# Experts: the first 64 tokens of an expert as two parts of 32, the second in a conditional block

## The chip, the cores and the metric

One core of a Trainium2 chip runs the whole program. The metric is the device time of one execution in microseconds (us); of the kernel before there are three timed executions, and one more was profiled.

## The reference, cut to what matters

The program is two transformer blocks in float32 over 512 tokens of width 1024. The change lies in the last part, the mixture of experts, which with the closing norm takes the last 1,400 of the 2,390 us:

```python
logits = xt @ router_w + router_b             # 512 tokens, 32 experts
top_val, top_idx = lax.top_k(logits, 4)       # each token goes to 4 experts
gate = softmax(top_val)
for e in range(32):                           # x: the tokens that chose e
    gu = x @ w_gu[e] + b_gu[e]                # 1024 -> 2 x 1024, the way up
    g, up = min(gu[:, :1024], 7), clip(gu[:, 1024:], -7, 7)
    act = (up + 1) * (g * sigmoid(1.702 * g))
    y = act @ w_down[e] + b_down[e]           # 1024 -> 1024, the way down
    out[tokens of e] += gate * y
```

The number of tokens of an expert depends on the data. The reference's router, worked out on its inputs, gives for experts 0 to 31: 41, 14, 111, 66, 75, 197, 45, 40, 14, 80, 57, 61, 46, 61, 26, 50, 62, 135, 185, 22, 73, 58, 101, 74, 62, 102, 1, 26, 39, 41, 12, 71. Seven have 32 or fewer, thirteen have 33 to 64, six have 65 to 96, three have 97 to 128 and three have more.

## The kernel before, in words

**Weights.** Each expert has twelve slabs of 1 MB: eight of `w_gu` (one for each 128 rows) and four of `w_down`. `load` issues them on SP into a ring of 21 slots in the order gu(0), gu(1), dn(0), gu(2), dn(1), and so on, two in flight (`FLIGHT`). A load waits until the last reader of its slot is done. Counting 21 back, the load of dn(e,1), the second slab of expert e's way down, goes to the slot of gu(e,0): it waits until TensorE has left the conditional block of expert e's way up. By then dn(e,0) and everything ahead of it may have been loaded. The load of gu(e+2,5) likewise waits for the end of the way down of expert e-1.

**Products.** Tokens are the stationary operand, weights the moving one. In form `n=2` (`up`, `down`) 64 tokens are loaded as 64 columns, and the two halves of the output columns go to two halves of the array and of PSUM's partitions. In form `n=4` 32 tokens are loaded, and four quarters of the output columns go to the four quarters of the array. Every float32 product is two records in the trace, so that a way up is 64 records of 512 columns in either form, and a way down 32 records of 512 columns (`n=2`) or 64 of 256 (`n=4`). A bias product opens each sum. `swiglu` follows on VectorE and ScalarE.

**Parts and blocks.** Tokens 0 to 63 of each expert go unconditionally in form `n=2`. Tokens 64 to 95 and 96 to 127 go in form `n=4`, inside `tc.If(r > 64)` and, nested in it, `tc.If(r > 96)`; later 64s (`chunk`) in form `n=2` inside further nested blocks. `r` is the expert's count in a register of each engine. For more than 128 tokens the activations of later chunks go to DRAM (`spill`) on the way up and are fetched back (`late<-spill`, line 1744) on the way down. `hinted` sets a branch hint for TensorE ahead of each block.

**Order.** For each e: `tile_up(e)` (line 1687), then the transposes of the next expert's tokens, then `tile_down(e-1)` (line 1739), then the transposes of expert e's activations. Inside a stretch without branches a scheduler sets the order; it put two or three of the four slabs of the way down of e-1 ahead of the block of the way up of e (line 1710). The block of the way down is at line 1742, its inner ones at 1748 and 1732.

**GpSimd.** Its queue holds, in program order, the gathers of tokens (`xg`, `x`, `late`), the spills and their way back, and the scatters `acc<-y` (line 1620) that add a part's result to the output. Each scatter waits for the landing of the one before.

Of the kernel before, what the change touches and what calls it, by code (L numbers as in the profile page):

```python
# [68 lines left out]
def uid(g, s):  # L69
    g.n += 1  # L70
    return f"{s}_{g.n}"
# [1245 lines left out]
NCH = T // CH  # L1317
QUARTERS = 2
RING = 5, 16
# [7 lines left out]
class Moe:  # L1327
# [143 lines left out]
    def table(self, n, half):  # L1471

        g = self.g
        nc, V = g.nc, g.nc.vector
        w, m = P // n, 4 if n == 2 else QUARTERS
        d = self.rp.tile([3 * NE, 4, 2, CH], F32, tag="dup", bufs=2, name=uid(g, "dup")).rearrange("p c h s -> p (c h s)")[:, :m * P].rearrange("p (c h s) -> p c h s", h=n, s=w)
        first = 0 if n == 2 else CH
        src = self.ptab[half][:3 * NE, first:first + m * w].rearrange("p (c s) -> p c s", s=w)
        (nc.scalar.copy if n == 2 else V.tensor_copy)(d, src.unsqueeze(2).to_broadcast([3 * NE, m, n, w]))
        pr = tr_tile(g, uid(g, "ptab"))  # L1480
        for c in range(m):
            nc.tensor.transpose(pr[:, c * 96:(c + 1) * 96], d[:, c].rearrange("p h s -> p (h s)"), g.ident[:96, :96])
        pv = pr[:, :m * 96].rearrange("p (c j e) -> p c j e", j=3, e=NE)
        cs = slice(half * 4, half * 4 + m)
        e = self.rp.tile([P, 4, NE], F32, tag="emp", bufs=2, name=uid(g, "emp"))[:, :m]
# [21 lines left out]
    def buffers(self, ctx):  # L1507
# [6 lines left out]
        tile = lambda name: self.pool.tile([P, 512], F32, name=name)  # L1514
        self.x1, self.act1 = tile("x1"), [tile(f"act1{j}") for j in range(2)]
        self.late, self.T = [[tile(f"{x}{j}") for j in range(2)] for x in ("late", "turned")]
        for x in (self.x1, *self.act1, *self.late):
            self.g.nc.gpsimd.memset(x, 0.0)
# [76 lines left out]

    def down(self, n, e, c, aT, mid=None):

# [6 lines left out]
        if n == 2:  # L1604
            nc.tensor.matmul(py, self.sel[e], self.bias[:, 2, :], start=True, stop=False)
        else:
            aT = aT[:, c * nb:(c + 1) * nb]
            for odd in range(2):
                nc.tensor.matmul(py, self.quarters(e, odd), self.bias[:, 2, odd * N:(odd + 1) * N], start=not odd, stop=False)
        for k in range(KD):  # L1610
# [78 lines left out]
    def tile_up(self, e, xT):  # L1689
# [3 lines left out]
        g, tc, r, x = self.g, self.g.tc, self.r[e], self.late  # L1693
        act0, act1 = self.pool.tile([P, 512], F32, tag="act0", bufs=1, name=uid(g, "act")), self.act1[e % 2]
        more = self.hinted(e, CH, "up")
        self.up(2, e, xT, act0, mid=lambda: self.transposed(self.x1, self.turned(1)))

# [11 lines left out]

        with tc.If(r > CH, label=more):  # L1710
            with tc.If(r > 2 * CH):
                self.fetch(x[0], e, 2)
            more = self.hinted(e, CH + CH // 2, "up")
            self.up(4, e, self.turned(1), act1[:, 0:256], 0)
            with tc.If(r > CH + CH // 2, label=more):
                more = self.hinted(e, 2 * CH, "up")
                self.up(4, e, self.turned(1), act1[:, 256:512], 1, mid=lambda: self.transposed(x[0], self.turned(2)))
                chunk(2, more)
        return act0, act1

    def tile_down(self, e, aT, act1, more):
        g, tc, r, a = self.g, self.g.tc, self.r[e], self.late
        self.down(2, e, 0, aT, mid=lambda: self.transposed(act1, self.turned(1), 0.5))

# [16 lines left out]

        with tc.If(r > CH, label=more):  # L1742
            with tc.If(r > 2 * CH):
                g.nc.gpsimd.dma_start(a[0], self.spill[e % 2, 0])
                back(3)
            more = self.hinted(e, CH + CH // 2, "down")
            self.down(4, e, 0, self.turned(1))
            with tc.If(r > CH + CH // 2, label=more):
                more = self.hinted(e, 2 * CH, "down")
                self.down(4, e, 1, self.turned(1), mid=lambda: self.transposed(a[0], self.turned(2), 0.5))  # L1750
                chunk(2, more)

# [44 lines left out]
    def run(self):  # L1797
# [11 lines left out]
        for e in range(NE + 1):  # L1809
# [4 lines left out]
            if e:  # L1814
                more = self.hinted(e - 1, CH, "down")
            if e + 1 < NE:
# [5 lines left out]
            if prev is not None:  # L1822
                self.tile_down(e - 1, aT, prev[1], more)
                blk = block()
                self.load(KD // 2)
# [119 lines left out]
```

## Time and profile before

| | us |
|---|---|
| three timed executions, median (lowest to highest) | 2384.4 (2382.29 to 2391.74) |
| profiled execution, its own time | 2391.75 |
| its span, first to last instruction | 2389.9 |
| TensorE busy in the span | 2083.4 (87%) |
| VectorE, ScalarE, GpSimd busy | 860.2, 476.2, 329.0 |
| bytes moved, mean rate | 584.26 MB, 244 GB/s |

The expert stage runs from about 980 us to the last product at 2356 us; the closing norm follows. TensorE is the busiest engine, but in most of the stage the queues that load weights are busy nine tenths too, so a share says little here: what matters is which of the two waits for the other at each expert.

### The profile page before, as it was taken

The numbers are of one execution on the slowest core, as the hardware profiler recorded it, in microseconds if no ns is written. First come the engines' busy times: TensorE is split into PE (matmuls) and PEld (weight loads), VectorE is DVE, ScalarE is ACT, GpSimd is POOL, SyncE is SP. The second block draws the span as 40 slices with busy tenths as digits, with TensorE's granted clock in tenths as the row PEclk, the third lists the DMA queues.
The fourth block names the chain that finished last, engine by engine and source line by source line (L and its number), as shares of the span: only waits on it lengthen the run. The fifth ranks groups of instructions, "written<-read, shape, count | busy, mean of one in ns | idle before, by whom it ended". The sixth has DMA issues, their size and how long they took to land. (4 is left out here: it accounts for less than half of the span.)

```text
span 2389.9 us, 31193 instructions
## 1 busy us (share of the span) xinstructions
PE 2083.4 (87%) x11589; PEld 1140.7 (48%) x11589; DVE 860.2 (36%) x1891; ACT 476.2 (20%) x839; POOL 329.0 (14%) x329
## 2 busy tenths in 40 slices
PE   6999888999989999798998888776887989888873
PEld 6756765688878978433333333222233333333221
DVE  6466668755566556411120111111121122121112
ACT  3345332234433134001001000000000000100001
POOL 2000224400022211101101101001001110101002
PEclk9999989999999999799999999999998999999997
DMA  6442476752336617879749899999966698989995
GB/s 190 121 162 69 154 191 198 222 173 98 97 117 219 208 50 254 348 292 325 278 152 332 291 338 335 323 354 335 340 236 243 235 331 326 332 312 340 346 333 180
DMA packets 213971, 584.26 MB, mean 244 GB/s; under 512 B 32287, under 2 KB 107438, under 8 KB 179822
## 3 DMA queue, kind: packets, MB, share of 16 engines
q1 hardware_dynamic: 182688, 523.74, 61.9%
q0 software_dynamic: 16784, 46.94, 7.2%
q10 hardware_dynamic: 14142, 9.10, 1.3%
q8 instruction: 190, 3.11, 0.5%
q14 instruction: 167, 1.37, 0.2%
HBM read 537.88 MB, written 41.84 MB: 243 GB/s over the span
## 5 line engine op out<-in xcount | busy, mean ns | idle before, releaser
L1587 PE MATMUL pg<-wgu,xT 128*64 128x512 f32 x1024 | 316.9, 648 | 57.2 <-issue 32.1
L1587 PE MATMUL pu<-wgu,xT 128*64 128x512 f32 x1024 | 299.0, 620 | 0.0
L1614 PE MATMUL py<-wdn,aT 128*64 128x512 f32 x1024 | 239.7, 605 | 21.4 <-DMA wdn<-in_exp_w_down 17.7
L1547 DVE TENSOR_TENSOR turned<-ptx,cols 128x512 f32<-128x512 f32 x42 | 29.0, 692 | 498.5 <-PE ptx L1539 497.2
L1561 ACT ACTIVATE th<-gm 128x512 f32<-128x512 f32 (+1 forms) x54 | 30.2, 559 | 843.6 <-DVE gm L1560 843.6
L89 DVE TENSOR_TENSOR wlo<-wst,whi 128x1024 fp32r<-128x1024 f32 (+1 forms) x109 | 136.6, 1253 | 124.7 <-ACT whi L88 115.7
L88 ACT CAST whi<-wst 128x1024 fp32r<-128x1024 f32 (+2 forms) x121 | 123.9, 1027 | 257.0 <-DMA wst<-in_w_ff_in 69.6
L1587 PEld LDWEIGHTS pg<-wgu,xT 128*64 128x64 f32 x1024 | 74.8, 145 | 191.7 <-issue 142.1
L1587 PEld LDWEIGHTS pu<-wgu,xT 128*64 128x64 f32 x1024 | 84.8, 144 | 159.7 <-issue 159.7
L1614 PEld LDWEIGHTS py<-wdn,aT 128*64 128x64 f32 x1024 | 70.0, 138 | 164.7 <-issue 130.1
L1620 POOL DMA_INDIRECT acc<-y,idx x54 | 85.7, 1586 | 327.3 <-ACTq L1742 137.8
L1591 PE MATMUL pgu<-wgu,turned 128*32 128x512 f32 x1152 | 129.2, 597 | 0.0
L98 PE MATMUL pf<-hTh,whi 128*128 128x512 f32 (+1 forms) x288 | 112.1, 393 | 8.0 <-ACT whi L88 5.0
L100 PE MATMUL pf<-hTh,wlo 128*128 128x512 f32 (+1 forms) x288 | 110.3, 385 | 6.6 <-DVE wlo L89 6.6
L1531 POOL DMA_INDIRECT xg<-hn,idx x32 | 32.9, 1028 | 600.7 <-PE ptx L1539 551.5
L1539 PE MATMUL ptx<-ident,act 128*128 128x128 f32 x256 | 44.4, 301 | 80.9 <-PEq L1742 52.8
L99 PE MATMUL pf<-hTl,whi 128*128 128x512 f32 (+1 forms) x288 | 110.4, 384 | 0.0
L1654 DVE CAST sel<-pick 128x128 fp32r<-128x128 f32 x32 | 7.6, 236 | 272.1 <-PEq L1732 133.2
L1614 PE MATMUL py<-wdn,turned 128*32 128x256 f32 (+1 forms) x1280 | 99.9, 414 | 0.0
L99 PE MATMUL plt<-wlo,ahi 128*128 128x512 f32 x256 | 99.7, 389 | 0.0
L98 PE MATMUL plt<-whi,ahi 128*128 128x512 f32 x256 | 99.6, 389 | 0.0
L100 PE MATMUL plt<-whi,alo 128*128 128x512 f32 x256 | 99.2, 389 | 0.0
(541 smaller groups left out, 3428.2 us busy)
## 6 DMA issues: line engine op xcount, KB each, us to landing
wgu<-in_exp_w_gu SPq DMA_DIRECT2D x256, 1024.0 KB
wdn<-in_exp_w_down SPq DMA_DIRECT2D x128, 1024.0 KB
wst<-in_w_in SPq DMA_DIRECT2D x36, 512.0 KB
wst<-in_w_ff_in SPq DMA_DIRECT2D x32, 512.0 KB
wst<-in_w_ff_out SPq DMA_DIRECT2D x32, 512.0 KB
ada_w<-in_ada_w SPq DMA_DIRECT2D x24, 512.0 KB
a<-in_ada_w SPq DMA_DIRECT2D x24, 512.0 KB
wst<-in_w_out SPq DMA_DIRECT2D x16, 512.0 KB
```

Of the source, the lines that this page charges most:

```text
L88: g.nc.scalar.copy(hi, st)
L89: eng.tensor_tensor(out=lo, in0=st, in1=hi.bitcast(F32), op=ALU.subtract)
L98: g.nc.tensor.matmul(out, ah, bh, start=start, stop=False)
L99: g.nc.tensor.matmul(out, ah, bl, start=False, stop=False)
L100: g.nc.tensor.matmul(out, al, bh, start=False, stop=stop)
L1531: self.g.nc.gpsimd.indirect_dma_start(out=x, out_offset=None, in_=self.hn, in_offset=bass.IndirectOffsetOnAxis(ap=self.idx[2][:, c, e:e + ...
L1539: d = g.nc.tensor.transpose(pt[:, b * P:(b + 1) * P], x[:, b * P:(b + 1) * P], g.ident)
L1561: nc.scalar.activation(th, gm, AF.Tanh, scale=0.851)
L1587: nc.tensor.matmul(ps[h * w:(h + 1) * w, :], lhs, W[k][:, o + h * N:o + (h + 1) * N], start=False, stop=(k == KD - 1))
L1591: nc.tensor.matmul(both[h * w:(h + 1) * w], lhs, wk[:, h], start=False, stop=(k == KD - 1))
L1614: nc.tensor.matmul(py[h * w:(h + 1) * w, :], lhs, W[k // 2][:, o:o + N], start=False, stop=(k == KD - 1))
L1620: nc.gpsimd.indirect_dma_start(out=acc, out_offset=bass.IndirectOffsetOnAxis(ap=self.idx[n][:, c, e:e + 1], axis=0), in_=y, in_offset=None ...
```

## The change

`QUARTERS` becomes 4, so that tables of row numbers and gates in form `n=4` cover tokens 0 to 127. Tokens 0 to 31 go unconditionally in form `n=4`; tokens 32 to 63 go in form `n=4` inside a new block `tc.If(r > 32)`, in which the block for more than 64 is now nested. The transposes of tokens 64 to 127 move into the new block. `act0` becomes one fixed tile that is cleared once. The first product of a way down gets an ordering edge behind the block of the way up. The diff without the tables:

```diff
-        act0, act1 = self.pool.tile([P, 512], F32, tag="act0", bufs=1, name=uid(g, "act")), self.act1[e % 2]
-        more = self.hinted(e, CH, "up")
-        self.up(2, e, xT, act0, mid=lambda: self.transposed(self.x1, self.turned(1)))
+        act0, act1 = self.act0, self.act1[e % 2]
+        more = self.hinted(e, CH // 2, "up")
+        self.up(4, e, xT, act0[:, 0:256], 0)
...
-        with tc.If(r > CH, label=more):
-            with tc.If(r > 2 * CH):
-                self.fetch(x[0], e, 2)
-            more = self.hinted(e, CH + CH // 2, "up")
-            self.up(4, e, self.turned(1), act1[:, 0:256], 0)
...
+        with tc.If(r > CH // 2, label=more):
+            more = self.hinted(e, CH, "up")
+            self.up(4, e, xT, act0[:, 256:512], 1, mid=lambda: self.transposed(self.x1, self.turned(1)))
+            with tc.If(r > CH, label=more):
+                with tc.If(r > 2 * CH):
+                    self.fetch(x[0], e, 2)
+                more = self.hinted(e, CH + CH // 2, "up")
+                self.up(4, e, self.turned(1), act1[:, 0:256], 0)
...
-        self.down(2, e, 0, aT, mid=lambda: self.transposed(act1, self.turned(1), 0.5))
+        self.down(4, e, 0, aT, after=after)
...
-        with tc.If(r > CH, label=more):
-            with tc.If(r > 2 * CH):
-                g.nc.gpsimd.dma_start(a[0], self.spill[e % 2, 0])
-                back(3)
...
+        with tc.If(r > CH // 2, label=more):
+            more = self.hinted(e, CH, "down")
+            self.down(4, e, 1, aT, mid=lambda: self.transposed(act1, self.turned(1), 0.5))
+            with tc.If(r > CH, label=more):
+                with tc.If(r > 2 * CH):
+                    g.nc.gpsimd.dma_start(a[0], self.spill[e % 2, 0])
+                    back(3)
...
-                more = self.hinted(e - 1, CH, "down")
+                more = self.hinted(e - 1, CH // 2, "down")
-                self.tile_down(e - 1, aT, prev[1], more)
+                self.tile_down(e - 1, aT, prev[1], more, blk)
```

In the changed kernel line 1712 opens the new block of the way up and 1715 the one for more than 64; 1747 and 1750 are the same two of the way down.

What the change moves, first on TensorE at the end of a way up. This is expert 2 before, from its last two slabs (`wgu`) to its block at 1710; `wdn` is the way down of expert 1:

```order
L1587 MATMUL pg_10000<-wgu_9133,xT_9660 64x512 x2
L1587 MATMUL pu_10001<-wgu_9133,xT_9660 64x512 x2
L1587 MATMUL pg_10000<-wgu_9135,xT_9660 64x512 x2
L1587 MATMUL pu_10001<-wgu_9135,xT_9660 64x512 x2
L1679 COMPARE_AND_BRANCH
L1679 UNCONDITIONAL_BRANCH x2
L1614 MATMUL py_10548<-wdn_9137,aT_9986 64x512 x4
L1614 MATMUL py_10548<-wdn_9641,aT_9986 64x512 x4
L1710 COMPARE_AND_BRANCH
```

Two slabs of the way down stand ahead of the block. The same place on TensorE in the changed kernel:

```order
L1590 MATMUL pgu_10150<-wgu_9181,xT_9752 32x512 x4
L1590 MATMUL pgu_10150<-wgu_9183,xT_9752 32x512 x4
L1712 COMPARE_AND_BRANCH
L1688 REGISTER_ALU
L1949 BRANCH_PREFETCH_HINT
L1580 MATMUL pgu_10196<-bias,sel_8530 128x512 x2
L1590 MATMUL pgu_10196<-wgu_8587,xT_9752 32x512 x4
L1590 MATMUL pgu_10196<-wgu_9171,xT_9752 32x512 x4
L1590 MATMUL pgu_10196<-wgu_9173,xT_9752 32x512 x4
```

No slab of a way down is left ahead of the block, and the second part with its own hint stands in it.

Next the way down of expert 1 on TensorE, behind that block. Before, from the hint for the block at 1742 to that block:

```order
L1941 BRANCH_PREFETCH_HINT
L1539 MATMUL ptx_10496<-ident,xg_9668 128x128 x4
L1539 MATMUL ptx_10560<-ident,act_8534 128x128 x4
L1614 MATMUL py_10548<-wdn_9643,aT_9986 64x512 x4
L1614 MATMUL py_10548<-wdn_9645,aT_9986 64x512 x4
L1742 COMPARE_AND_BRANCH
```

Eight products (sixteen records) and eight transposes part the hint and its branch. In the changed kernel, up to the second hint:

```order
L1949 BRANCH_PREFETCH_HINT
L1538 MATMUL ptx_10691<-ident,xg_9760 128x128 x4
L1608 MATMUL py_10743<-bias,sel_8531 128x256 x2
L1616 MATMUL py_10743<-wdn_9185,aT_10137 32x256 x8
L1616 MATMUL py_10743<-wdn_9733,aT_10137 32x256 x8
L1616 MATMUL py_10743<-wdn_9735,aT_10137 32x256 x8
L1616 MATMUL py_10743<-wdn_9737,aT_10137 32x256 x8
L1747 COMPARE_AND_BRANCH
L1688 REGISTER_ALU
L1949 BRANCH_PREFETCH_HINT
```

All four slabs (32 products, 64 records of half the width) now stand between the hint and the branch, and the transposes of `act` have gone into the block.

Last the queue of GpSimd at the way down of expert 0, from the gather for expert 2 to the fetch that brings spilled activations back (`late<-spill`). Before:

```order
L1531 DMA xg_9668<-hn,idx_7703 128x512
L1620 DMA acc<-y_9696,idx_7703 1152x512
L1742 COMPARE_AND_BRANCH
L1743 COMPARE_AND_BRANCH
L1728 COMPARE_AND_BRANCH
L1729 DMA late_8536<-spill 128x512
L1728 UNCONDITIONAL_BRANCH
L1728 ISA
L1728 UNCONDITIONAL_BRANCH
L1744 DMA late_8535<-spill 128x512
```

One scatter stands ahead of the fetches. In the changed kernel:

```order
L1530 DMA xg_9760<-hn,idx_7703 128x512
L1622 DMA acc<-y_9799,idx_7704 2304x256
L1747 COMPARE_AND_BRANCH
L1622 DMA acc<-y_9847,idx_7704 2304x256
L1750 COMPARE_AND_BRANCH
L1751 COMPARE_AND_BRANCH
L1733 COMPARE_AND_BRANCH
L1734 DMA late_8539<-spill 128x512
L1733 UNCONDITIONAL_BRANCH
L1733 ISA
L1733 UNCONDITIONAL_BRANCH
L1752 DMA late_8538<-spill 128x512
```

Two scatters stand ahead of them now.

## Rows read from the trace of the kernel before

**Rows 1.** The page: busy share of the DMA engines in 40 equal slices, in tenths.

```profile
DMA  6442476752336617879749899999966698989995
```

**Rows 2.** Waits of SP's queue, 880 to 2390 us: total us, times, longest.

```profile
SPq L1632 <- DMA wgu<-in_exp_w_gu: 554.9, 187, 5.7
...
SPq L1635 <- PEq L1699: 78.8, 5, 36.9
```

**Rows 3.** Timeline of TensorE, expert 5's way up: start, us, instruction, [idle before].

```profile
1177.85 0.65 PE L1539 MATMUL ptx<-ident,act 128*128 128x128 f32 x4 [0.65 <-PEq L1748]
...
1178.57 0.40 PE L1574 MATMUL pg<-bias,sel 128*128 128x512 f32 x1
...
1179.13 1.08 PE L1587 MATMUL pg<-wgu,xT 128*64 128x512 f32 x4
...
1180.90 1.03 PE L1587 MATMUL pg<-wgu,xT 128*64 128x512 f32 x4
...
1193.96 3.60 PE L1614 MATMUL py<-wdn,aT 128*64 128x512 f32 x16
1197.49 0.73 PE L1581 MATMUL pgu<-bias,sel 128*128 128x512 f32 x2
...
1205.15 0.73 PE L1581 MATMUL pgu<-bias,sel 128*128 128x512 f32 x2
```

**Rows 4.** Timeline of TensorE, expert 2's way down.

```profile
1118.15 0.63 PE L1539 MATMUL ptx<-ident,act 128*128 128x128 f32 x4 [0.73 <-DVEq L1715]
...
1122.30 0.51 PE L1609 MATMUL py<-bias,sel 128*128 128x256 f32 x2
...
1126.33 0.51 PE L1609 MATMUL py<-bias,sel 128*128 128x256 f32 x2
...
1136.23 1.11 PE L1539 MATMUL ptx<-ident,act 128*128 128x128 f32 x4 [5.08 <-PEq L1732]
```

**Rows 5.** Waits of TensorE, 960 to 2390 us: total us, times, longest.

```profile
PE ptx L1539 <- PEq L1742: 52.8, 20, 4.6
PE pg L1587 <- issue: 32.1, 14, 4.6
...
PE ptx L1539 <- DMA late<-spill: 14.4, 2, 10.5
...
PE ptx L1539 <- PEq L1732: 12.3, 6, 5.1
...
PE ptx L1539 <- PEq L1748: 3.3, 5, 0.7
```

**Rows 6.** Line 1742: TensorE's branches there, ns min/median/max.

```profile
L1742 PEldq COMPARE_BRANCH  x32: 67/4540/7377, 1028.8 to 2347.7; - x32
```

**Rows 7.** Timeline of TensorE after the jump at 1742 in expert 1.

```profile
1087.77 1.98 PE L1587 MATMUL pg<-wgu,xT 128*64 128x512 f32 x4
...
1091.24 1.21 PE L1587 MATMUL pg<-wgu,xT 128*64 128x512 f32 x4
```

**Rows 8.** TensorE in that stretch: window, us, busy (instructions), granted clock, DMA share, GB/s.

```profile
1085.50:1089.00 3.50, 3.50 (x11) 0.50 1.01 272
```

**Rows 9.** Timeline of GpSimd, expert 17's way down: scatter, fetch back, scatter.

```profile
1812.25 1.62 POOL L1620 DMA_INDIRECT acc<-y,idx  x1 [0.30 <-issue]
1813.97 0.61 POOL L1744 DMA_DIRECT2D late<-spill  x1
1821.89 1.62 POOL L1620 DMA_INDIRECT acc<-y,idx  x1 [7.31 <-DMA acc<-y,idx]
```

**Rows 10.** Timeline of TensorE, expert 17's way up, from its last wait for weights.

```profile
1695.32 1.57 PE L1587 MATMUL pg<-wgu,xT 128*64 128x512 f32 x4 [3.99 <-DMA wgu<-in_exp_w_gu]
...
1702.89 0.74 PE L1581 MATMUL pgu<-bias,sel 128*128 128x512 f32 x2
```

**Rows 11.** Timeline of GpSimd, the last two scatters of the program (expert 31).

```profile
2353.61 1.55 POOL L1620 DMA_INDIRECT acc<-y,idx  x1 [11.04 <-ACT y L1618]
2359.28 1.55 POOL L1620 DMA_INDIRECT acc<-y,idx  x1 [4.12 <-DMA acc<-y,idx]
```

More of the change, by code (lines that the diff above doesn't have):

```diff
@@ L1317 @@
 NCH = T // CH
-QUARTERS = 2
+QUARTERS = 4
 RING = 5, 16
@@ L1474, in table @@
         nc, V = g.nc, g.nc.vector
[L1475 to L1478, printed above, removed]
+        w, m = P // n, 4
+        d = self.rp.tile([3 * NE, 4, 2, CH], F32, tag="dup", bufs=2, name=uid(g, "dup")).rearrange("p c h s -> p (c h s)").rearrange("p (c h s) -> p c h s", h=n, s=w)
+        src = self.ptab[half][:3 * NE, :m * w].rearrange("p (c s) -> p c s", s=w)
         (nc.scalar.copy if n == 2 else V.tensor_copy)(d, src.unsqueeze(2).to_broadcast([3 * NE, m, n, w]))
@@ L1484, in table @@
         cs = slice(half * 4, half * 4 + m)
-        e = self.rp.tile([P, 4, NE], F32, tag="emp", bufs=2, name=uid(g, "emp"))[:, :m]
+        e = self.rp.tile([P, 4, NE], F32, tag="emp", bufs=2, name=uid(g, "emp"))
         V.tensor_scalar(e, pv[:, :, 0, :], 0.0, self.empty[n], op0=ALU.is_equal, op1=ALU.mult)
@@ L1514, in buffers @@
         tile = lambda name: self.pool.tile([P, 512], F32, name=name)
-        self.x1, self.act1 = tile("x1"), [tile(f"act1{j}") for j in range(2)]
+        self.x1, self.act0, self.act1 = tile("x1"), tile("act0"), [tile(f"act1{j}") for j in range(2)]
         self.late, self.T = [[tile(f"{x}{j}") for j in range(2)] for x in ("late", "turned")]
-        for x in (self.x1, *self.act1, *self.late):
+        for x in (self.x1, self.act0, *self.act1, *self.late):
             self.g.nc.gpsimd.memset(x, 0.0)
@@ L1594, in up, with down @@
         self.swiglu(act, pg, pu, N)
-    def down(self, n, e, c, aT, mid=None):
+    def down(self, n, e, c, aT, mid=None, after=None):
         g = self.g
@@ L1604, in down @@
         if n == 2:
-            nc.tensor.matmul(py, self.sel[e], self.bias[:, 2, :], start=True, stop=False)
+            d = nc.tensor.matmul(py, self.sel[e], self.bias[:, 2, :], start=True, stop=False)
         else:
-            aT = aT[:, c * nb:(c + 1) * nb]
+            aT = aT[:, c % 2 * nb:(c % 2 + 1) * nb]
             for odd in range(2):
-                nc.tensor.matmul(py, self.quarters(e, odd), self.bias[:, 2, odd * N:(odd + 1) * N], start=not odd, stop=False)
+                x = nc.tensor.matmul(py, self.quarters(e, odd), self.bias[:, 2, odd * N:(odd + 1) * N], start=not odd, stop=False)
+                d = d if odd else x
+        if after is not None:
+            behind(g, d, after)
         for k in range(KD):
@@ L1708, in chunk, with tile_down @@
                     chunk(c + 1, more)
-        with tc.If(r > CH, label=more):
-            with tc.If(r > 2 * CH):
-                self.fetch(x[0], e, 2)
-            more = self.hinted(e, CH + CH // 2, "up")
-            self.up(4, e, self.turned(1), act1[:, 0:256], 0)
[L1715 to L1718, printed above, removed]
+        with tc.If(r > CH // 2, label=more):
[6 more added lines that the diff above has]
+                self.up(4, e, self.turned(1), act1[:, 0:256], 0)
+                with tc.If(r > CH + CH // 2, label=more):
+                    more = self.hinted(e, 2 * CH, "up")
+                    self.up(4, e, self.turned(1), act1[:, 256:512], 1, mid=lambda: self.transposed(x[0], self.turned(2)))
+                    chunk(2, more)
         return act0, act1
-    def tile_down(self, e, aT, act1, more):
+    def tile_down(self, e, aT, act1, more, after):
         g, tc, r, a = self.g, self.g.tc, self.r[e], self.late
-        self.down(2, e, 0, aT, mid=lambda: self.transposed(act1, self.turned(1), 0.5))
+        self.down(4, e, 0, aT, after=after)
         def back(c):
@@ L1740, in chunk @@
                     chunk(c + 1, more)
-        with tc.If(r > CH, label=more):
-            with tc.If(r > 2 * CH):
-                g.nc.gpsimd.dma_start(a[0], self.spill[e % 2, 0])
-                back(3)
[L1746 to L1751, printed above, removed]
+        with tc.If(r > CH // 2, label=more):
[5 more added lines that the diff above has]
+                    back(3)
+                more = self.hinted(e, CH + CH // 2, "down")
+                self.down(4, e, 2, self.turned(1))
+                with tc.If(r > CH + CH // 2, label=more):
+                    more = self.hinted(e, 2 * CH, "down")
+                    self.down(4, e, 3, self.turned(1), mid=lambda: self.transposed(a[0], self.turned(2), 0.5))
+                    chunk(2, more)
     def turned(self, c):
```

## The prediction

> **What bounds the kernel now.** I read the page first, then the waits of SP's queue, then those of TensorE, then single stretches. The page's slices show the DMA engines at seven to nine tenths through most of the stage, with two dips: slices 20 and 21 (about 1135 to 1255 us, experts 4 and 5) and 30 to 32 (about 1733 to 1912 us, experts 17 to 20) [rows 1]. SP's waits say the same: 554.9 us for the landing of an earlier `wgu` load, the normal pace, against 78.8 us in five waits for TensorE to leave a block of chunks past 128 tokens [rows 2]. So there are two regimes. Where experts are light the weights set the pace, TensorE waits for slabs, and work taken from it gives nothing. Where experts are heavy the ring is full and the load of dn(e,1) stands until TensorE has left the way up of e; there a microsecond on TensorE is a microsecond of the run. Following the issue of dn(e,1) against the end of that block, I take two such stretches: **A**, from the start to the way up of expert 7, and **B**, from the way up of expert 17, in which the last long wait for weights lies, to that of expert 25. After the last load there is a short tail on TensorE and GpSimd. Only A, B and the tail are summed. Of the seven experts with 32 tokens or fewer, five (8, 14, 26, 27, 30) lie where the loads set the pace; only experts 1 (in A) and 19 (in B) can pay.
>
> **The change part by part.** *Products up.* In form n=2 a way up takes 1193.96 - 1178.57 = 15.4 us, the transposes for the next 64 tokens included; one part of 32 takes 1205.15 - 1197.49 = 7.7 us [rows 3]. So two parts and 0.6 of transposes take 15.9: an expert above 32 pays +0.5, one at or below gains 7.7. A: experts 0 and 2 to 7 pay 3.5, expert 1 gives -7.7. B: experts 18 and 20 to 25 pay 3.5, expert 19 gives -7.7.
>
> *Products down.* In form n=2: 0.5 bias, twice 3.6 (two slabs each, [rows 3]) and 0.6 transposes, 8.3 us; in form n=4 a part takes 1126.33 - 1122.30 = 4.0 [rows 4], two with the transposes 8.7. Above 32: +0.4, otherwise -4.3. A (ways down 0, 2 to 5, and 1): +2.0 and -4.3. B (16 to 18, 20 to 23, and 19): +2.8 and -4.3.
>
> *Slabs moved behind the block.* Two slabs of the way down of e-1 stood ahead of the block of e, 3.6 us [rows 3]. Behind it, the slots of e come free 3.6 us sooner, and the 3.6 us are paid right after. Inside a stretch that cancels, at its last block it is a gain: A -3.6, B -3.6. At the start of B it is the other way round: the slabs were done while 17's block had not begun, now they follow, +3.6.
>
> *Cover that is lost.* With loads setting the pace, all of the n=2 form lay beside loads, and the tail behind the last slab was short. Now only the first part does, the second follows when all eight slabs are there. It is hidden by the loads of the next four slabs, except where a stretch begins: from the last wait to the first part past 64 took 1702.89 - 1695.32 = 7.6 us [rows 10]; now it is the rest of part one (about 1.6 at the low clock) and 8.3 of part two, 9.9: +2.4 in B. Without any cover it would be 7.7.
>
> *Blocks.* Entering a block cost nothing to be seen; leaving one by a jump does. For up to 64 tokens the jump at 1742 left TensorE idle 52.8 us in 20 cases, 2.6 each [rows 5]; the branch itself took 4.5 us in the median and up to 7.4 [rows 6], part of it beside queued products. [...] And there was a second stall within the first slab, 32.1 us in all [rows 5], about 1.6 per jump. Together 6.1. The jumps at 1748 cost 3.3 us in five, 0.7 each [rows 5], those at 1732 12.3 in six, one of them 5.08 [rows 4, 5]. I put the difference down to how far the hint is ahead: the hint of 1748 has all of a first part behind a queue of older products, that of 1742 little. In the changed kernel both ways out (1747 for up to 32, 1750 for up to 64) have one part between hint and branch and short products in the queue, like 1732. Bounds: all short, 0.7, or all as bad as the worst 1732 with what follows, 5.1 + 1.9 + 1.6 = 8.6, plus a page more. I take two long in three, 5.1 on average as a mean of these, 1.0 less than before. A has two (experts 0, 1), B three (16, 19, 21): -2 and -3.
>
> [...]
>
> *Small things on TensorE.* The way out of the inner block of a way up costs 0.3 more than out of the outer: +0.9 in A, +0.6 in B. The wait for VectorE of 0.73 ahead of the transposes of `act` [rows 4] goes, since these now stand in the block: about -2.9 in A (four heavy experts), -4.3 in B (five, two of them with longer waits).
>
> *GpSimd.* A second scatter now stands ahead of the fetch of spilled activations, and a scatter waits for the landing of the one before: 1821.89 - 1812.25 = 9.6 us here, 5.7 in the quiet tail [rows 9, 11]. Queued behind it are that fetch, and behind the fetch the later scatters and the next gathers. TensorE already waits for the fetch, 14.4 us in two cases [rows 5]. The first scatter comes 3.6 us or so sooner, as the part is shorter. With 8 us between scatters that leaves +4.4 for experts 5 (A) and 18 (B); at 17 the first scatter was held up otherwise and will not come sooner: +8.5. Bounds for each are 0, if the earlier first scatter makes up for it, and 9.6. The other extra scatters and the later gather of tokens 64 to 127 (now behind the block) have a whole way down and a part up as cover, over 11 us against a landing of some 8; without it each would cost a few us. The new table columns, the cleared tile and SP's extra branches cost nothing: they lie beside the loads already in flight, 3 to 4 us apart.
>
> *Tail.* Expert 31 has 71 tokens: three scatters in a row now, two before. The first comes about 3.3 sooner, then 5.67 apart [rows 11]: last one at 2353.61 - 3.3 + 2 x 5.67 = 2361.65 against 2359.28, +2.4; with the uncovered second part up of 31, +3. Bounds 0 and 8.
>
> Sum. A: 3.5 - 7.7 + 2.0 - 4.3 - 3.6 - 2 + 0.9 - 2.9 + 4.4 = -9.7. B: 3.5 - 7.7 + 2.8 - 4.3 - 3.6 + 3.6 + 2.4 - 3 + 0.6 - 4.3 + 4.4 + 8.5 = +2.9. Tail +3. Total -3.8 us. The profiled execution took 2391.75 us, 7.35 above the median of 2384.4; the sum is a difference and is carried to the median: 2384.4 - 3.8 = 2380.6, about **2381**.
>
> **The rivals.** *Short jumps.* If the hints are just far enough ahead, the five jumps in A and B cost 0.7 instead of 5.1: 22 us less, 2381 - 22 = 2359; with three of five, 2368. For it: one of three jumps at 1732 right behind a part of this length was short. Against: the other two were not. *Long jumps.* If the branch always arrives before the hint's fetch, each of the five costs 8.6 and a second fetch of 1.6 more, about 10 instead of 5.1: +24, 2405; at +4 each 2401, slower than before. It decides from about 3.5 us per jump above my value. For it: the queue ahead of these branches holds shorter products than before, so less hides the fetch. [...] *The loads hide it.* If A is shorter than I read, or the loads catch up inside it, its gain goes and B's loss stays: 2384.4 + 2.9 + 3 = 2390, still no change that can be told. *It doesn't save what it says.* If quarters of the array did not run side by side, a part would take 15 us; the parts past 64 show 7.7, so I give it nothing.
>
> **How the numbers follow.** A measurement of this kernel tells about 0.5%, 12 us, from no change: faster is below 2372, slower above 2396. My sum 0.45 (its own range 2370 to 2392), loads hide it 0.10, short jumps 0.23, long jumps 0.15, and 0.07 for something unseen, half on each side. Faster: 0.23 and 0.04, some of the sum's lower edge, 0.28. Slower: 0.14 and 0.04, 0.18. Same: 0.54. The range reaches into both jump cases: 2361 to 2402.
>
> **What would show it.** Parts of 7.7 and 4.0 us in both places; for experts 1 and 19 ways up of 7.7; blocks without slabs of a way down ahead. Idle time of TensorE behind 1747 and 1750: 0.7 to 5 each, summed over 20 experts against 52.8; this decides between the jump cases. TensorE's wait for `late<-spill` above 14.4. SP's waits for TensorE lower in A, about equal in B. Three scatters at the end 5.7 apart. I am wrong if stretches of light experts change their length, for the loads should set that alone.

## The result and the profile after

The change made the kernel slower: 2397.7 us against 2378.2 (medians of 20 executions of each), ratio 1.0073 with a 95% interval of 1.0048 to 1.0098, or +17 us. The ratio leaves out two slowed executions of the changed kernel, so it is a little below that of the medians. The forecast was -4 us, no change that can be told. The measured time lies within 2361 to 2402, the direction is the other one. The two profiled executions differ by less, 2402.26 against 2391.75, and the parts below are parts of that difference of 10.5.

Waits of TensorE in the changed kernel, 960 to 2400 us (total us, times, longest), beside [rows 5]:

```profile
PE ptx L1538 <- DVE sel L1657: 72.6, 27, 5.7
...
PE ptx L1538 <- DMA late<-spill: 24.6, 2, 14.0
PE ptx L1538 <- issue: 16.9, 6, 8.4
PE ptx L1538 <- PEq L1747: 10.9, 3, 4.7
PE pgu L1590 <- DVE turned L1547: 9.4, 1, 9.4
```

The first row is the wait that [rows 5] puts down to `PEq L1742` and `L1748`: the transposes of `act` behind a way down. The profile names `sel` here because VectorE writes it last, but VectorE itself waits there for TensorE's sequencer to leave the block (`DVE sel L1656 <- PEq L1750: 132.1, 13` and `PEq L1756: 67.3, 5`). Summed over the ways out of 30 ways down (experts 0 to 29), TensorE was idle 82.7 us; before it was 67.1 in the same 30. A "way out" is the jump that leaves the blocks of an expert's way down. Third row: 8.4 us of it is a third wait for `late` (expert 5), for which the profile found no releaser. The last row is new.

SP's wait for TensorE to leave the chunks past 128, beside 78.8 in [rows 2]; the ring stands longer in the heavy stretches than before:

```profile
SPq L1637 <- PEq L1701: 98.0, 6, 44.1
```

The way out of expert 3 (66 tokens) on TensorE, beside the first rows of [rows 3], where the same way out took 0.65:

```profile
1164.33 3.66 PE L1616 MATMUL py<-wdn,turned 128*32 128x256 f32 x64
1173.72 1.09 PE L1538 MATMUL ptx<-ident,act 128*128 128x128 f32 x4 [5.73 <-DVE sel L1657]
1174.46 1.20 PE L1580 MATMUL pgu<-bias,sel 128*128 128x512 f32 x2
1175.59 7.69 PE L1590 MATMUL pgu<-wgu,xT 128*32 128x512 f32 x64
```

The new wait, in the way up of expert 18: TensorE, then VectorE, then GpSimd's scatters:

```profile
1758.62 0.73 PE L1580 MATMUL pgu<-bias,sel 128*128 128x512 f32 x2
1768.72 3.64 PE L1590 MATMUL pgu<-wgu,turned 128*32 128x512 f32 x16 [9.36 <-DVE turned L1547]
```

```profile
1765.59 0.42 DVE L1559 TENSOR_SCALAR gm<-pgu 128x256 f32<-128x256 f32 x1 [23.66 <-DMA acc<-y,idx]
```

```profile
1745.97 1.62 POOL L1622 DMA_INDIRECT acc<-y,idx  x1 [0.30 <-issue]
1755.86 1.56 POOL L1622 DMA_INDIRECT acc<-y,idx  x1 [8.27 <-issue]
```

`swiglu` takes its two buffers (`gm`, `th`) from the pair that also holds `y`, which the scatters read. The second scatter of expert 16, issued at 1755.86, holds one of them until it has landed; VectorE stands at `gm` until 1765.59, the transposed tokens 64 to 127 (`turned`) queue behind it, and TensorE waits for these. Over the stage VectorE waits for this 126 us; in the kernel before 4.8.

```profile
DVE gm L1559 <- DMA acc<-y,idx: 126.3, 9, 23.7
```

GpSimd in expert 17's way down, beside [rows 9]: now two scatters ahead of the fetch, which goes out at 1825.83.

```profile
1815.60 1.62 POOL L1622 DMA_INDIRECT acc<-y,idx  x1 [0.30 <-issue]
1823.92 1.56 POOL L1622 DMA_INDIRECT acc<-y,idx  x1 [6.69 <-ACT y L1620]
1825.83 0.61 POOL L1752 DMA_DIRECT2D late<-spill  x1 [0.34 <-issue]
```

The end, beside [rows 11]: three scatters 4.7 and 4.6 us apart.

```profile
2360.87 1.56 POOL L1622 DMA_INDIRECT acc<-y,idx  x1 [10.06 <-ACT y L1620]
2365.56 1.56 POOL L1622 DMA_INDIRECT acc<-y,idx  x1 [3.12 <-ACT y L1620]
2370.18 1.56 POOL L1622 DMA_INDIRECT acc<-y,idx  x1 [3.06 <-DMA acc<-y,idx]
```

By stretch, read at the issue of dn(e,1): A ends 4.0 us later (forecast -9.7); from there to expert 16 the changed kernel gains 9.3; B loses 21.9 (forecast +2.9); from expert 25 to 31 it gains 8.0, and the tail costs 2.0 (forecast +3).

TensorE in A and B, from the issue of dn(0,1) to that of dn(7,1) and from dn(16,1) to dn(25,1): window, us, busy (instructions), granted clock, DMA share, GB/s. The first two rows are the kernel before, the last two the changed one.

```profile
984.90:1335.70 350.80, 317.24 (x1874) 0.95 0.78 278
1695.40:2119.60 424.20, 378.43 (x2374) 0.95 0.81 290
985.70:1339.70 354.00, 309.02 (x2836) 0.93 0.77 275
1690.10:2136.20 446.10, 380.43 (x3608) 0.93 0.78 278
```

### The profile page after: what moved, and what is told of

It reads as the page before. It is cut to its first block, busy times and chain, and to the rows that moved or that the text cites. A ratio compares the mean times of both kernels' runs of the same rounds, so it can differ in the third digit from the quotient of the medians.

```text
span 2400.5 us, 40635 instructions
## 1 busy us (share of the span) xinstructions
PE 2055.5 (86%) x15888; PEld 1157.5 (48%) x15891; DVE 853.9 (36%) x1977; ACT 480.7 (20%) x882; POOL 370.5 (15%) x355
## 5 line engine op out<-in xcount | busy, mean ns | idle before, releaser
L1590 PE MATMUL pgu<-wgu,xT 128*32 128x512 f32 x3648 | 467.5, 651 | 51.9 <-DMA wgu<-in_exp_w_gu 42.6
L1590 PEld LDWEIGHTS pgu<-wgu,xT 128*32 128x32 f32 x3648 | 112.7, 117 | 358.6 <-issue 269.2
L1616 PE MATMUL py<-wdn,aT 128*32 128x256 f32 x3648 | 229.0, 396 | 16.1 <-DMA wdn<-in_exp_w_down 9.2
L1559 DVE TENSOR_SCALAR gm<-pgu 128x256 f32<-128x256 f32 x75 | 31.8, 424 | 554.4 <-PE pgu L1590 290.8
L1622 POOL DMA_INDIRECT acc<-y,idx x79 | 124.7, 1579 | 452.5 <-ACT y L1620 151.1
L1560 ACT ACTIVATE th<-gm 128x256 f32<-128x256 f32 (+1 forms) x79 | 33.8, 427 | 775.7 <-DVE gm L1559 775.7
L1616 PEld LDWEIGHTS py<-wdn,aT 128*32 128x32 f32 x3648 | 113.0, 113 | 104.7 <-issue 26.2
L1656 DVE CAST sel<-pick 128x128 fp32r<-128x128 f32 x32 | 7.8, 245 | 396.2 <-PEq L1737 164.1
L1590 PE MATMUL pgu<-wgu,turned 128*32 128x512 f32 x1152 | 131.3, 605 | 9.4 <-DVE turned L1547 9.4
L1530 POOL DMA_INDIRECT xg<-hn,idx x32 | 32.1, 1004 | 435.1 <-PE ptx L1538 374.7
L1620 ACT ACTIVATE y<-py,gate 128x256 f32<-128x256 f32 (+1 forms) x79 | 38.3, 484 | 283.1 <-PE py L1616 229.6
L1538 PEld LDWEIGHTS ptx<-ident,act 128*128 128x128 f32 x228 | 27.8, 158 | 113.1 <-PEq L1750 42.5
```

The costliest lines, as they stand in the source:

```text
L1530: self.g.nc.gpsimd.indirect_dma_start(out=x, out_offset=None, in_=self.hn, in_offset=bass.IndirectOffsetOnAxis(ap=self.idx[2][:, c, e:e + ...
L1538: d = g.nc.tensor.transpose(pt[:, b * P:(b + 1) * P], x[:, b * P:(b + 1) * P], g.ident)
L1560: nc.scalar.activation(th, gm, AF.Tanh, scale=0.851)
L1590: nc.tensor.matmul(both[h * w:(h + 1) * w], lhs, wk[:, h], start=False, stop=(k == KD - 1))
L1616: nc.tensor.matmul(py[h * w:(h + 1) * w, :], lhs, W[k // 2][:, o:o + N], start=False, stop=(k == KD - 1))
L1620: nc.scalar.mul(y, py, self.gate[n][:, c, e:e + 1])
```

## The experiments

All ratios are to the kernel before, with 95% intervals. The diffs show only the lines that matter. The first four part the change.

**e1**, only the way up in quarters. The way down has the form `n=2` for tokens 0 to 63; ScalarE writes `aT` in the order that this form wants.

```diff
-        self.down(4, e, 0, aT, after=after)
+        self.down(2, e, 0, aT, mid=lambda: self.transposed(act1, self.turned(1), 0.5), after=after)
-        with tc.If(r > CH // 2, label=more):
-            more = self.hinted(e, CH, "down")
-            self.down(4, e, 1, aT, ...)
```

> Only the way up in two parts of 32; the way down keeps its form of 64 columns with its blocks, one scatter per 64 tokens, behind the block of the way up as in the changed kernel. Theory 1 (the loss comes from the way down: later exits, one more scatter ahead of the fetches): ratio to the kernel before 0.996 to 1.002, no TensorE wait for late<-spill above 16 us in two or three cases, exits of experts 3, 4 and 20 about 0.7 us. Theory 2 (the loss comes from the second part of the way up standing behind a block, uncovered): ratio 1.005 to 1.008.

**e2**, only the way down in quarters; it reads `aT` in the order that the form `n=2` left it in.

```diff
-        more = self.hinted(e, CH // 2, "up")
-        self.up(4, e, xT, act0[:, 0:256], 0)
+        more = self.hinted(e, CH, "up")
+        self.up(2, e, xT, act0, mid=lambda: self.transposed(self.x1, self.turned(1)))
-        with tc.If(r > CH // 2, label=more):
-            self.up(4, e, xT, act0[:, 256:512], 1, ...)
```

> Only the way down in two parts of 32; the way up keeps its form of 64 columns. Theory 1: all of the loss is here and the gain of two short ways up (7.7 us each on the path) is not: ratio 1.007 to 1.012, waits for late<-spill 20 us or more, exits past 65 to 96 tokens 2 to 6 us each. Theory 2: ratio 0.998 to 1.002.

**e3**, the kernel before with the ordering edge alone.

```diff
+            if after is not None:
+                behind(g, d, after)
-                self.tile_down(e - 1, aT, prev[1], more)
+                self.tile_down(e - 1, aT, prev[1], more, blk)
```

> The kernel before with one edit: the first product of a way down is ordered behind the block of the way up. Theory 1 and the forecast's term: two slabs (3.6 us) moved, -4 us to 0, ratio 0.998 to 1.000. Rival: the moved products are what lengthens the change (cover of the first slab lost): ratio 1.003 or more.

**e4**, the changed kernel with an earlier fetch.

```diff
         with tc.If(r > CH // 2, label=more):
+            with tc.If(r > 2 * CH):
+                g.nc.gpsimd.dma_start(a[0], self.spill[e % 2, 0])
+                back(3)
             more = self.hinted(e, CH, "down")
```

> The changed kernel, with the fetch of spilled activations at the head of the block for more than 32 tokens, so that one scatter stands ahead of it and not two. If the second scatter delays the fetch: the waits for late<-spill fall from 35 us in three cases to 18 or less, ratio to the kernel before 1.000 to 1.004 instead of 1.007. If the fetch is late for another reason (spill, engine of the transfer), the waits stay above 28 us and the ratio at 1.006 to 1.009.

Measured: e1 0.9865 (0.9827 to 0.9902), e2 0.9898 (0.9862 to 0.9934), **e3 0.9836** (0.9793 to 0.9878), e4 1.0022 (0.9989 to 1.0054). The expectations of e1 to e3 all missed: the edge, which had a term of -3.6 us in the forecast, is worth 39 us when it is put into the kernel before. Against e3, quarters on the way up cost 0.3% and on the way down 0.6%, about the width of an interval; both together cost 2.4%. So neither half is the loss; most of it appears when they meet. In e4 the wait for `late` falls from 8.4 to 0.9 us for expert 5, is gone for 18 and falls from 14.0 to 9.5 for 17: the second scatter ahead of the fetch was the cause of what the change had added.

In e3 these rows of the waits of TensorE and SP and, for TensorE's branches at the way out past 64 tokens (ns min/median/max), of the line answer to [rows 5, 2, 6]:

```profile
PE ptx L1539 <- PEq L1744: 18.2, 20, 3.4
```

```profile
SPq L1637 <- PEq L1701: 51.5, 2, 36.4
```

```profile
L1744 PEldq COMPARE_BRANCH  x32: 68/1102/6341, 1028.3 to 2301.6; - x32
```

52.8 us of idle time fell to 18.2. All slabs of the way down now stand between hint and branch. From this came theory 3: a way out costs by the distance from its hint to its branch, that is the time from the hint's record to the branch's.

**e5** was to bring the hint of e3 close to its branch again. **e6** and **e7** give hints of the changed kernel earlier. **e8** parts the buffers.

```diff
 e5  hint inside down(), behind five of eight slices
 e6 -                more = self.hinted(e - 1, CH // 2, "down")
    +                more = [self.hinted(e - 1, n, "down") for n in (CH // 2, CH)]
 e7 +            third = self.hinted(e, CH + CH // 2, "down")
                 more = self.hinted(e, CH, "down")
 e8 -        gm, th = (self.pool.tile([P, 512], F32, tag="y", bufs=2, ...)[:, :n] for x in ("gm", "th"))
    +        gm, th = (self.G[:, 0:256], self.G[:, 256:512]) if n == 256 else (self.G, pg)
    -        y = self.pool.tile([P, 512], F32, tag="y", bufs=2, name=uid(g, "y"))[:, :N]
    +        y = self.Y if n == 2 else self.Y[:, c % 2 * 256:c % 2 * 256 + 256]
```

> As e3 (the kernel before, way down behind the block of the way up), but the hint for the exit past 64 tokens is given inside the way down, behind five of its eight slices, so that the branch follows it by some 1 to 2 us as before, not by 5.4. Theory 3 (e3 gained by the distance between hint and branch): TensorE's idle time at these 20 exits goes back from 18 us to 45 or more, ratio to the kernel before 0.994 to 1.003. Rival (e3 gained because slots of the ring come free sooner): exits may be long, the ratio stays at 0.980 to 0.988.

> The changed kernel, with the hint for the exit of 33 to 64 tokens given together with the one for 32 or fewer, one part (4 us) earlier. Theory 3: branch 8 us or more behind its hint, idle time at these thirteen exits 0.8 us each instead of 0.8 to 5.6, ratio to the kernel before 0.992 to 1.001 against 1.007 of the changed kernel. Rival (only one hint can be pending): exits of 32 or fewer grow or stay at 3 to 5 us, those of 33 to 64 don't shrink, ratio 1.004 to 1.012.

> The changed kernel, with the hint for the exit of 65 to 96 tokens given at the head of the second part (ahead of the hint for 64), one part earlier. Theory 3: the branch comes 8 us behind its hint instead of 3.5, idle time of experts 3, 4, 9, 20 and 23 about 0.7 each instead of 5.7, 3.3, 1.3, 1.7 and 2.9, ratio 1.001 to 1.005. Rival (one pending hint): those exits unchanged, ratio 1.005 to 1.010.

> The changed kernel, with the two buffers of swiglu apart from the buffers that the scatters read, in the same space. If swiglu of expert 18 waited for a scatter to land: TensorE's wait of 9.4 us for turned<-ptx there is gone and VectorE no longer waits for acc<-y ahead of gm; ratio 1.002 to 1.006 instead of 1.007. If the scatter only happened to land then: the wait stays, ratio 1.005 to 1.009.

Measured: e5 0.9817 (0.9785 to 0.9849), e6 1.0064 (1.0034 to 1.0094), e7 1.0092 (1.0056 to 1.0128), e8 1.0006 (0.9980 to 1.0033). e5 says nothing on hints: the scheduler put the hint back to the head of the way down, so it is e3 once more. e6 and e7 missed, and tell nothing on theory 3 either: of two hints given one behind the other only one is in the trace. The changed kernel has 158 hints of TensorE, e6 133 and e7 146:

```profile
L1949 PEldq BRANCH_PREFETCH_HINT  x158: 27/33/44, 967.0 to 2363.8; - x158
L1948 PEldq BRANCH_PREFETCH_HINT  x133: 28/33/44, 967.9 to 2375.2; - x133
L1949 PEldq BRANCH_PREFETCH_HINT  x146: 27/33/44, 966.3 to 2365.7; - x146
```

With both hints e6 would have 165 and e7 171: one is missing at each of the 32 ways down of e6, and in each of the 25 blocks past 32 tokens of e7. In e7 the branches for 33 to 64 tokens still take 3.6 us and those for 65 to 96 5.2, near the 5.6 without a hint (e16), so the earlier hint seems to be the one that is missing. In e6 the branches take 4.9 us up to 32 tokens and 5.1 for 33 to 64, against 5.6 and 5.5 without hints (e16), and which hint is left is open. Whether a hint outlives another branch in between is not shown by any run. e8 took the wait of expert 18 away, and VectorE's wait for scatters ahead of `gm` with it: 0.7%, nearly the whole loss. The trace shows 9.4 of these some 16 us as a wait of TensorE; where the rest lies is not shown.

**e9** takes the hint past 64 tokens out of e3, **e10** the edge out of the changed kernel; **e11** has the edits of e4 and e8; **e12** makes the second part of the way down unconditional.

```diff
 e9  -                more = self.hinted(e - 1, CH, "down")
     +            more = None
 e10 -                self.tile_down(e - 1, aT, prev[1], more, blk)
     +                self.tile_down(e - 1, aT, prev[1], more, None)
 e12          self.down(4, e, 0, aT, after=after)
     +        self.down(4, e, 1, aT, mid=lambda: self.transposed(act1, self.turned(1), 0.5), after=after)
     -        with tc.If(r > CH // 2, label=more):
```

> As e3, without any hint for the exit past 64 tokens (in e5 the scheduler had put the hint back to the head of the way down, so that its distance had not changed). Theory 3 (the distance of the hint is what e3 gained): the branch takes 5 to 6 us at each of the 20 exits, TensorE idle 45 us or more there against 18, ratio to the kernel before 0.993 to 1.002. Rival (slots come free sooner): ratio 0.980 to 0.988 whatever the exits take. In between: both have a share.

> The changed kernel without its ordering edge: slabs of the way down stand ahead of the block of the way up again. Theory 3: the edge is worth little here, since the exit of 33 to 64 tokens has its own hint one part (4 us) ahead either way; only exits of 32 or fewer get 1 to 2 us longer and the 3.6 us of two slabs return: ratio to the kernel before 1.007 to 1.014. If the edge is worth as much as in the kernel before (1.6%): ratio 1.020 or more.

> The changed kernel with both edits, the earlier fetch of e4 and the own buffers of e8. If the two waits are separate, their gains add up: 1.0073 less 0.005 less 0.007, ratio 0.993 to 0.998, and what is left to e3's 0.984 lies in the exits, whose idle time stays at 75 us or more over all thirty. If they are one wait seen twice: ratio 1.000 or more.

> The changed kernel, with the second part of the way down unconditional: one block and one exit less, hint and exit past 64 tokens parted by two parts (8 us) and not one. Theory 3: the idle time at the exits of up to 64 tokens falls to about 1 us each, the 4 us more for the five light experts in load-paced stretches cost nothing, ratio to the kernel before 0.988 to 0.996. Rival (the two scatters and two parts of the way down cost, not its exits): ratio 1.004 or more.

Measured: e9 0.9891 (0.9855 to 0.9927), e10 1.0112 (1.0070 to 1.0154), e11 0.9969 (0.9946 to 0.9993), e12 1.0169 (1.0142 to 1.0197). e9 lies between the two theories: a third of the edge's gain goes with the hint, the rest is the order. (The intervals of e9 and e3 overlap; against e5, which has the same order as e3, the hint is worth 0.7%.) In e10 the edge is worth 0.4%, which is within the noise, and not 1.6%. In e11 the two waits add up (1.0% together). e12 missed: its ways out up to 64 tokens did shorten, the time rose by 1%. TensorE's waits there and, in the second fence, VectorE's:

```profile
PE ptx L1538 <- PEq L1748: 29.5, 20, 4.5
PE ptx L1538 <- PEq L1754: 20.7, 5, 6.0
```

```profile
DVE gm L1559 <- DMA acc<-y,idx: 255.1, 17, 19.9
```

The ways out past 64 tokens stayed long (L1754), and every expert now has a second scatter for which `swiglu` waits.

**e13** is e12 with the buffers of e8, **e14** the kernel before without its hint past 64 tokens, **e15** e1 with the buffers of e8, **e16** the changed kernel without the three hints of the way down, **e17** the same of e11.

```diff
 e14 -                more = self.hinted(e - 1, CH, "down")
     +            more = None
 e16 -                more = self.hinted(e - 1, CH // 2, "down")
     +            more = None
     -            more = self.hinted(e, CH, "down")
     +            more = None
     -                more = self.hinted(e, CH + CH // 2, "down")
     +                more = None
```

> e12 (second part of the way down unconditional) with the own buffers of e8. It differs from e8 only in the block for more than 32 tokens. If e12 was slow because swiglu waited for the scatters of the second part (VectorE waited 255 us for acc<-y there against 126): that wait goes, and with exits of up to 64 tokens at 1.5 us instead of 2.9 the ratio to the kernel before is 0.992 to 1.000, at or below e8's 1.0006. If two scatters at every expert cost by themselves (the next gathers and fetches queue behind them): 1.006 to 1.016.

> The kernel before without the hint for the exit past 64 tokens. Theory 3: the hint stands 0.4 to 4 us ahead of its branch there, too close to help; ratio 0.998 to 1.003, idle time at the 20 exits 48 to 62 us against 52.8. Rival (any hint helps as much as in e3, 0.55%): ratio 1.004 to 1.008, idle time 70 us or more.

> e1 (only the way up in parts of 32, with the ordering edge) with the own buffers. If swiglu's wait for scatters held e1 back too (VectorE's wait for turned costs TensorE 5.9 us in three cases there): ratio 0.981 to 0.985, level with e3 or better. If not: 0.985 to 0.990 as e1.

> The changed kernel without the three hints of the way down (past 32, 64 and 96 tokens). If a hint 3 to 4.5 us ahead still brings more than it costs (branches there take 3.6 to 3.9 us in the mean against 5.6 close behind a hint): ratio to the kernel before 1.010 to 1.016, idle time at the thirty exits 100 us or more against 83. If it costs as in the kernel before: ratio 1.000 to 1.004, and the second stalls behind the exits (13 us) go. Neither: 1.005 to 1.010, the exits' hints are no part of the loss.

> e11 (earlier fetch, own buffers) without the three hints of the way down: the same difference as from the changed kernel to e16, on 0.997: 1.000 to 1.006 if hints at this distance help, 0.990 to 0.994 if they harm, 0.995 to 0.999 if neither.

Measured: e13 1.0074 (1.0047 to 1.0101), e14 **0.9951** (0.9921 to 0.9981), e15 0.9954 (0.9927 to 0.9980), e16 1.0153 (1.0110 to 1.0197), e17 1.0047 (1.0022 to 1.0071). e13 came out as its second reading: own buffers bring 0.95% to e12 too, but a second part and a second scatter at every expert leave it 0.7% behind e8. e14 missed both expectations: without its hint the kernel before is faster. Its waits beside [rows 5]:

```profile
PE ptx L1539 <- PEq L1742: 48.6, 20, 4.1
```

```profile
PE pg L1587 <- issue: 0.4, 1, 0.4
PE pg L1587 <- DMA wgu<-in_exp_w_gu: 50.9, 35, 3.8
```

The ways out are nearly as long as with the hint (52.8), but the second stall within the first slab, 32.1 us in 14 cases, is gone. Of these 32.1 us 10.5 lay in A and B; the wait of the same products for weights rises from 23.3 to 50.9, all of it outside A and B, where the loads set the pace and take up what the stall leaves. That the hint makes the stall is not general, though; in e9, without a hint too, it is there:

```profile
PE pg L1587 <- issue: 25.4, 11, 4.1
```

In e15 the wide `y` has one buffer left and ScalarE waits 122 us for scatters, so that e15 tells nothing about e1. e16 and e17 agree: the hints of the changed kernel, some 3 to 5 us ahead of their branches, are worth 0.8%. Without them, in e16:

```profile
PE ptx L1538 <- DVE sel L1657: 126.1, 30, 6.8
```

What the ways out up to 64 tokens (19 of them, without that of expert 30) show in the records of hints, branches and products, as means in us; the distance is from hint to branch, "queued" is how long TensorE still has products when the branch starts:

| kernel | distance | branch takes | queued | idle, sum |
|---|---|---|---|---|
| before | 2.3 | 5.4 | 3.1 | 51.5 |
| e14, before without hint | none | 5.3 | 3.2 | 47.1 |
| e9, edge without hint | none | 4.9 | 2.9 | 46.1 |
| e3, edge | 7.8 | 2.6 | 2.8 | 17.8 |
| e1, way up in quarters | 4.9 | 2.9 | 4.2 | 9.7 |
| changed | 4.3 | 3.9 | 1.4 | 59.7 |
| e16, changed without hints | none | 5.5 | 1.4 | 90.4 |
| e6, one of two hints left | 7.6 from the one | 5.1 | 1.5 | 81.6 |
| e12, straight second part | 8.7 | 2.4 | 1.4 | 29.0 |

The means hide a wide spread: in e3 ten of the nineteen stand 5.4 to 5.5 us behind their hints, and these branches take from 1.7 to 6.3 us. Distance shortens a branch in the mean; it does not fix its length.

## Why the prediction was wrong, by its steps

**The step that failed** is "The other extra scatters and the later gather of tokens 64 to 127 [...] have a whole way down and a part up as cover, over 11 us against a landing of some 8": a term put at nothing. The forecast counted who queues behind a scatter on GpSimd and not who waits for the buffer that the scatter reads. What the runs showed in its place is `swiglu` waiting for that buffer: 9.4 us of TensorE's time at expert 18, and 0.7% or some 16 us over the run (e8). The second scatter goes out 9.9 us behind the first and lands 7.6 us later, so the buffer is held for 17.5 us and not for 8. With buffers apart the ratio is 1.0006, the "no change" of the forecast. It was not the only miss. The terms of A and B beside TensorE's waits in the two profiled executions, in us:

| term | forecast | shown |
|---|---|---|
| products and slabs moved (TensorE's busy time) | -15.8 | -6.2 |
| jumps | -5 | +0.1 |
| VectorE ahead of the transposes of `act` | -7.2 | -8.1 |
| ends of the way up | +1.5 | +8.5 |
| fetch of spilled activations | +17.3 | +15.3 |
| `swiglu` behind a scatter | 0 | +9.4 |
| cover that is lost; the rest | +2.4 | +6.1 |
| sum | -6.8 | +25.1 |

The stretches between gained 17.3 that were not forecast, without which the time would have been further off: that the measured time lies within the range at all is in part luck.

**The edge.** The forecast gave the moved slabs -3.6 in A and nothing in B. In the kernel before, the edge alone is worth 39 us (e3). Its two parts can be told apart by taking the hint away on both sides: from e14 to e9, without hints, the order is worth 0.6%, about 14 us, against some -11 in the forecast (-3.6 for the slabs, -7 for VectorE's 0.7 us waits, which the edge removes and which the forecast put down to the new block). The hint turns from a loss of 0.5% (e14) into a gain of 0.55% (e9 to e3), because the whole way down in form `n=2` now parts it from its branch (7.8 us against 2.3, table). Each of these differences is about as wide as its own interval. The forecast priced the jump of the changed kernel, and never asked what the edge alone would do to the jump of the kernel before. That is no reason for the loss, since the changed kernel has the edge too; it tells how much the rest of the change gave away.

**Jumps.** The forecast had them 1.0 us cheaper each for experts up to 64 and left the heavier ones alone. Its own bounds give no such gain: "two long in three" of 8.6 and one of 0.7 are 6.0 in the mean, not 5.1, against 6.1 before. Shown for up to 64 tokens: the distance grew from 2.3 to 4.3 us, which took 1.5 us from the branch; the products queued behind it are half as long, which took 1.7 us of cover away (table). So the idle time at the way out rose a little, from 51.5 to 59.7 us. That is the argument of the rival *Long jumps*, "the queue ahead of these branches holds shorter products than before", and it held, though at a smaller price than its 10. The ways out for 65 to 96 tokens, which had no term, went from 0.7 us [rows 5, `L1748`] to 3.0 on average, 5.7 for expert 3: their hint still stands one part ahead, but fewer products are queued when it is given, so that the branch follows after 3.5 us instead of 5.7. For experts 3 and 4, in A, this was +7.8 us. Against it, the second stall within the first slab became rarer, 32.1 us before [rows 5] and 6.5 after (`PE pgu L1590 <- issue`). In A and B together the ways out cost 9.1 more and the second stall 9.0 less. The 1.9 us within the forecast's 6.1 and 8.6 no run shows as such; what the trace of before shows is 3.5 us for the eight first products behind one jump, against 1.8 [rows 7, 3], at a granted clock of 0.50 [rows 8].

The two traces show what the long branches end behind: packets on DMA queue 8, `q8 instruction: 190, 3.11` on the page of the kernel before, all of 16 KB. Of TensorE's branches 30 took over 1 us before and 37 after. Each of them ends 2.3 us or more behind the start of such a packet, 2.5 us in the median before (at most 4.1) and 2.4 after (at most 2.7). In 25 of either kernel the packet starts inside the branch; in the other 5 and 12, of 1.1 to 2.1 us, it starts ahead of it. Of the 14 second stalls of [rows 5] 11 (29.0 of the 32.1 us) end 2.2 to 2.7 us behind the start of such a packet too. The branches without a hint took 5.5 us in e16 and 5.3 in e14, those with one 4.3 to 8.7 us ahead of them 2.4 to 3.9 (changed, e1, e3 and e12 in the table). That a hint brings the packet forward fits these numbers; no run parts it from the rest.

**Products.** The lengths of the parts held, 7.7 and 4.0 us. But TensorE's busy time changed by -8.2 us in A (forecast -10.1) and +2.0 in B (forecast -5.7). Part of this is the clock, which the forecast priced only behind jumps: the granted clock of A and B fell from 0.95 to 0.93. By the trace's clock records TensorE was busy at the lower of their two levels, 0.50, for 57.3 us of A and B before and for 67.1 after; at half speed that is an estimated 5 us of work lost. No run changes the clock by itself.

**GpSimd.** The fetch of spilled activations cost +4.5 for expert 5 (forecast 4.4), +3.5 for 17 (8.5) and +7.3 for 18 (4.4): 15.3 against 17.3. This term was right in mechanism and, by errors at 17 and 18 that cancel, in its sum; e4 shows its cause. The scatters put at nothing are the step that failed. With the first part of the way up only 7.7 us long, `swiglu` comes for the buffer 7.7 us sooner. An early `swiglu` alone makes VectorE wait 183 us (e1), of which 5.9 reach TensorE, a second scatter alone 17 us (e2), of which none do:

```profile
DVE gm L1570 <- DMA acc<-y,idx: 183.2, 14, 20.7
DVE gm L1559 <- DMA acc<-y,idx: 17.0, 2, 8.9
```

That the two together make the wait of 9.4 us at expert 18 fits these rows; no run parts them further.

**Ends of the way up.** Forecast +0.9 and +0.6; TensorE's idle time there, ahead of the transposes of the next expert's tokens, grew from 4.2 to 8.8 us in A and from 4.5 to 8.4 in B.

**Light experts' stretches.** "The loads should set that alone" failed too: they were 9.3 and 8.0 us shorter after than before, in single executions. Had they not been, the result would be worse. What sets their pace beside the loads stays open.

**What is left.** e3 plus the two halves would give 0.993, the changed kernel has 1.007. Of these 1.5 points the wait for the buffer is 0.7 (e8). The late fetch is worth 0.5 (e4), but its wait stands in e2 too (32.7 us against 33.0 in the changed kernel), so it belongs to the way down and not to the meeting of the two halves. e11, without both, lies 1.3% above e3; its thirty ways out leave TensorE idle 87 us against 38. In the profiled executions A and B together are 41 us longer in e11 than in e3, and the ways out take 23 of them. That they make the 1.3% is argued, not shown: e12 and e13, made to shorten them, became slower, with a part of 4 us more for light experts, more scatters and long ways out past 64 tokens in the same edit.

The version to keep is e3: the edge alone, 1.6% faster than the kernel before and 2.4% faster than the changed one.

## What to carry to other kernels

When a change contains an ordering edge beside its main idea, price the edge alone on the old kernel: here it was the best part and was spent on the rest. For every conditional block look at two times together, the distance from hint to branch and the work still queued when the branch starts; halving the length of products halved the cover here, from 3.1 to 1.4 us. Count the hints in the trace as well: of two given one behind the other, one was missing (133 in e6 and 146 in e7, where 165 and 171 were given). For every added asynchronous store ask who needs its source buffer next, not only who queues behind it.

## What was not expected of the hardware

- A taken branch of TensorE without a hint took 4.9 to 5.5 us in the mean (table). With one, over the kernels before, changed, e1 to e4 and e8, its mean fell with the distance of the hint: 5.6 us below 2.6 us of distance (14 ways out), 3.9 from 2.6 to 4 (40), 3.6 from 4 to 4.9 (84), 2.6 from 4.9 to 5.6 (16), 1.1 from 5.6 to 7 (22), 0.6 from 7 to 9 (22); farther than 9 it was either below 0.5 or about 4, but for one (12). Two kernels made later bear it out less well: at 7 to 9 us e12 has 2.5 (16) and e13 1.6 (20).
- Of two hints given one behind the other only one is in the trace (133 in e6 and 146 in e7, against 158).
- The hint of the kernel before, 2.3 us ahead of its branch in the mean, made it 0.5% slower than none (e14).
